# Both S5 layers in finer steps, in a written order for two engines

## The chip, the cores and the metric

The kernel runs on one core of a Trainium2 chip. A core has TensorE (PE, with weight loads listed as PEld), VectorE (DVE), ScalarE (ACT), GpSimd (POOL) and SyncE (SP); each takes its instructions from a queue of its own, in order. SP, ACT and POOL also issue DMAs, and a DMA that waits holds what stands behind it in that queue. The metric is the device time of one execution in microseconds (us).

## The reference

A trunk of four layers over 256 tokens of width 1024 in fp32. Layer i mixes tokens by i mod 3: an S5 state-space layer (layers 0 and 3), forgetting attention (FoX, layer 1), gated linear attention (GLA, layer 2). Each layer is

```python
h += mixer(rmsnorm(h))
h += square(relu(rmsnorm(h) @ w1)) @ w2
h += (p[i] @ W_pp) * sigmoid(rmsnorm(h) @ W_pg)      # PLE
```

and the S5 mixer is

```python
u = xn @ w_in                               # 64 groups of 16 channels
dt = exp(log_dt); ab = exp((lr + 1j * li) * dt)
bbar = (ab - 1) / (lr + 1j * li) * b
s[t] = ab * s[t - 1] + bbar @ u[t]          # 64 complex states a group
y = real(c @ s) + d * u
z1, z2 = split(gelu(y) @ w_glu, 2)
out = (z1 * sigmoid(z2)) @ w_out
```

## The kernel before

Activations lie transposed, features on partitions and the 256 tokens on the free axis. `self.HH` holds h in four tiles of two feature blocks each. A dense product multiplies weights and activations that are split into a high and a low part: `unit` loads 512 KB of weights over SP, ACT makes the high part (L157), VectorE the low part (L159), and `col` issues three matmuls (L173 to L175). A unit is 24 such matmuls. `dense` walks the units of a block of 512 outputs and hands the sums to `evac`. `lo_after` lets a low part wait for an instruction.

**The S5 layer** (`s5`) works in four blocks b of 256 channels (8 pairs of groups). A block's work is:

- w: its part of w_in (`block`, or in layer 0 `plain_block` with plain fp32 weights, L261); then u (L1068), scaled by the row's inverse root mean square `r`; `s5_inputs` spreads u with eight small DMAs, four on SP and four on ACT (L963).
- i: the weights that lead into the states. Layer 0 makes them from `bT` and a table of powers `coef` (L867 to L869), after a rotation `rot` (`s5_rot`, L889 to L892) and the decay `d0` (L1081, L1082).
- o: the weights that lead out (`s5_way_out`, L907 to L911), and `s5_inside`: a small product on TensorE (k, L927 to L932), copied by ACT and spread to `tm`, the lags inside four tokens, by four DMAs on ACT (L942).
- s: `s5_states`: matmuls into the states (L977), rotation (L984 to L986), scan (L989), rotation back (L991 to L1003).
- y: `s5_outputs`: matmuls out (L1015), GELU on ACT, four transposes (L1027) and the split of the result into `g` (L267 on ACT, L268 on VectorE).

In layer 3 the weights of i and o come from DRAM, where `s5_ahead` has put them piece by piece during the MLPs of layers 0 to 2. `s5_scalars` computes the small quantities, as a generator in steps; `s5_table` sends the table to DRAM on POOL's queue and `s5_fetch` brings coef, bT and `bc` back. Step p is `plain_ple_proj` (layer 0) or `ple_proj` (layer 3): the PLE projection of p[i].

The order in which these are traced is the string `FIRST` (layer 0) or `LATER` (layer 3). The last two y are traced inside the first part of the gate. That order isn't the order of execution: the tile framework's planner, which has modelled costs, places each engine's instructions by what it expects to be ready, so steps of several blocks interleave. After the states comes the gate: `dense` for the third block of 512 outputs (`right`: sigmoid on ACT), then the first (`left`: product and split into `m`), then the fourth and the second; then `out_proj`.

PSUM has eight banks, as `acc` (3), `wk` (3), `po` (1) and `mk` (1). Other buffers are counted in `BUFS`.

## Time and profile before

| | us |
|---|---|
| median of 3 runs | 1458.47 |
| lowest, highest | 1456.15, 1462.42 |
| the profiled execution | 1462.34 |
| its span, first to last instruction | 1460.6 |
| S5, layer 0: until the last w_out matmul | 187.4 |
| S5, layer 3: from its first w_in matmul | 1092 to 1239.6 |
| mean granted TensorE clock | 0.982 |

In the profile's tables a group of instructions is named by engine, line, what it writes and reads, and its count. "Idle before" is the time that the engine stood still just ahead of it, with what released it. The ends of matmuls are modelled, since they are pipelined, so TensorE's busy time overstates its work where they are few and small; the start of one step and the start of the next are the better measure.

### The profile page before, as it was taken

How to read it: one execution, taken by the hardware profiler on the slowest of the kernel's cores; microseconds unless marked ns; L12 is line 12 of the kernel's file. 1: busy time of each engine (PE TensorE's matmuls, PEld its weight loads, DVE VectorE, ACT ScalarE, POOL GpSimd, SP SyncE). 2: the span in 40 equal slices, each digit the busy share in tenths (PEclk: the TensorE clock that was granted, in tenths of full speed). 3: DMA queues.
4: the chain of work that ended last, by engine and by line, in shares of the span. 5: the costliest groups of instructions: out<-in, count | busy, mean ns of one | idle time of the engine just before them, and what ended most of it. 6: DMA issues, size and time to landing. Idle time of an engine off the chain costs nothing.

```text
span 1460.6 us, 26531 instructions
## 1 busy us (share of the span) xinstructions
PE 1402.0 (96%) x10734; PEld 1265.4 (87%) x10734; DVE 1050.7 (72%) x1657; ACT 717.5 (49%) x1110; POOL 89.3 (6%) x146
## 2 busy tenths in 40 slices
PE   7799999999999999999999999999997899999998
PEld 6689988889999888888989588888997899888898
DVE  8795578766876678776676468877677856766665
ACT  3133565445655655445566455444463335545453
POOL 4100000001000000010004000100000000000020
PEclk9889999999999999999999999999999899999999
DMA  6634656656654356775655445766665446566561
GB/s 208 191 89 132 181 175 192 189 167 207 191 155 140 122 154 197 242 229 175 186 170 156 134 130 187 229 211 207 204 233 152 145 130 185 181 188 187 173 195 66
DMA packets 146347, 255.06 MB, mean 175 GB/s; under 512 B 24768, under 2 KB 35296, under 8 KB 146224
## 3 DMA queue, kind: packets, MB, share of 16 engines
q1 hardware_dynamic: 132912, 234.35, 52.4%
q0 software_dynamic: 5248, 17.31, 3.7%
q10 hardware_dynamic: 8064, 1.71, 0.6%
q8 instruction: 84, 1.38, 0.4%
q14 instruction: 39, 0.32, 0.1%
HBM read 242.68 MB, written 7.86 MB: 172 GB/s over the span
## 4 chain that ended last, share of the span: by engine, by line
PE 61%; DVE 4%; DMA 2%; ACT 1%; issue 1%; DVEq 0%; POOLq 0%; SPq 0%; ACTq 0%
PE wk L209 8%; PE acc L209 7%; PE acc L173 4%; PE acc L174 4%; PE acc L175 4%; PE wk L211 4%; PE wk L173 4%; PE wk L175 4%; PE wk L174 4%; PE acc L211 3%; PE mk L209 3%; PE po L209 2%; DMA raw<-mlp_w 2%; DVE wlo L159 1%; PE acc L234 1%; PE acc L233 1%
## 5 line engine op out<-in xcount | busy, mean ns | idle before, releaser
L159 DVE TENSOR_TENSOR wlo<-raw,whi 128x1024 fp32r<-128x1024 f32 x406 | 493.6, 1226 | 293.1 <-ACT whi L157 287.5
L157 ACT CAST whi<-raw 128x1024 fp32r<-128x1024 f32 x406 | 421.6, 1049 | 466.1 <-DMA raw<-mlp_w 84.7
L209 PE MATMUL wk<-x,whi 128*128 128x512 f32 x576 | 181.5, 400 | 8.3 <-DVE relu L220 8.3
L211 PEld LDWEIGHTS wk<-x,wlo 128*128 128x128 f32 x576 | 106.4, 190 | 22.8
L209 PE MATMUL acc<-s,whi 128*128 128x512 f32 x384 | 117.7, 395 | 0.0
L211 PE MATMUL wk<-x,wlo 128*128 128x256 f32 x576 | 113.2, 280 | 0.0
L209 PEld LDWEIGHTS wk<-x,whi 128*128 128x128 f32 x576 | 91.8, 191 | 12.3 <-DVE relu L220 9.2
L173 PE MATMUL acc<-x,whi 128*128 128x256 f32 x352 | 99.8, 287 | 1.8 <-DVE u L1068 1.0
L175 PE MATMUL acc<-x,wlo 128*128 128x256 f32 x352 | 100.1, 286 | 0.7 <-DVE wlo L159 0.7
L174 PE MATMUL acc<-x,whi 128*128 128x256 f32 x352 | 99.4, 285 | 0.0
L211 PEld LDWEIGHTS acc<-s,wlo 128*128 128x128 f32 x384 | 69.7, 188 | 15.8 <-DVE wlo L159 0.5
L209 PE MATMUL mk<-x,whi 128*128 128x512 f32 x256 | 81.6, 395 | 0.0
L211 PE MATMUL acc<-s,wlo 128*128 128x256 f32 x384 | 74.3, 281 | 0.1
L175 PE MATMUL wk<-s,wlo 128*128 128x256 f32 x256 | 72.4, 283 | 0.0
L174 PE MATMUL wk<-s,whi 128*128 128x256 f32 x256 | 72.4, 283 | 0.0
L173 PE MATMUL wk<-s,whi 128*128 128x256 f32 x256 | 72.4, 283 | 0.0
L173 PEld LDWEIGHTS acc<-x,whi 128*128 128x128 f32 x352 | 66.9, 191 | 3.3 <-ACT pp L436 1.3
L175 PEld LDWEIGHTS acc<-x,wlo 128*128 128x128 f32 x352 | 67.2, 191 | 1.5 <-DVE wlo L159 1.2
L174 PEld LDWEIGHTS acc<-x,whi 128*128 128x128 f32 x352 | 67.2, 192 | 0.3
L209 PEld LDWEIGHTS acc<-s,whi 128*128 128x128 f32 x384 | 59.7, 189 | 1.6
L209 PE MATMUL po<-s,whi 128*128 128x512 f32 x192 | 60.5, 395 | 0.6 <-DVE y L220 0.6
L209 PE MATMUL wk<-s,whi 128*128 128x512 f32 x192 | 59.6, 395 | 0.0
(398 smaller groups left out, 3368.5 us busy)
## 6 DMA issues: line engine op xcount, KB each, us to landing
raw<-mlp_w SPq DMA_DIRECT2D x256, 512.0 KB, 4.1
raw<-s_w_glu SPq DMA_DIRECT2D x32, 512.0 KB, 3.9
raw<-ple_gate SPq DMA_DIRECT2D x32, 512.0 KB, 3.9
raw<-fox_w_in SPq DMA_DIRECT2D x24, 512.0 KB, 3.8
raw<-gla_w_in SPq DMA_DIRECT2D x24, 512.0 KB, 3.6
raw<-s_w_out SPq DMA_DIRECT2D x16, 512.0 KB, 3.7
kept<-kept SPq DMA_DIRECT2D x12, 512.0 KB, 4.0
raw<-s_w_in SPq DMA_DIRECT2D x11, 512.0 KB, 3.5
```

What stands on the lines that cost most here:

```text
L157: nc.scalar.copy(hi, raw)
L159: self.last_lo = nc.vector.tensor_tensor(lo, raw, hi.bitcast(F32), ALU.subtract)
L173: mm(ps, hi, x[:, 0], start=first, stop=False, skip_group_check=True)
L174: mm(ps, hi, x[:, 1], start=False, stop=False, skip_group_check=True)
L175: self.last_mm = mm(ps, lo, x[:, 0], start=False, stop=last, skip_group_check=True)
L209: mm(ps[n], hi[:, i, s], v[i], start=first and i == 0, stop=False, skip_group_check=True)
L211: self.last_mm = mm(ps[n][:, 0], lo[:, i, s], v[i][:, 0], start=False, stop=last and i == UK - 1, skip_group_check=True)
L233: mm(ps[half], a[:, 0, t], hi[:, k], start=k0 + k == 0, stop=False)
L234: mm(ps[half], a[:, 0, t], lo[:, k], start=False, stop=False)
```

## The change

- `in_order`, a context, links all instructions that are traced inside it on the named engines, each to the one before on the same engine, so that the planner keeps the traced order. `s5` wraps the steps of both layers in it for PE and DVE. ACT, POOL and SP are placed by the planner as before. A few ACT instructions at layer 0's start (the scaled x, the squares and the first steps of the scalars) stand in an order of their own.
- The steps are cut finer: w in halves of a block (w0 to w7), with the weight split of layer 3 as a step (h); u; c (x and squares), n (mean squares), z (inverse root and the rest of the scalars); f and q (fetches), r (rot and decay), i, o, k; x (matmuls into the states), s (rotation and scan), e (rotation back); y, t (transposes, high part), g (low part).
- The gate's right half is no longer done by `dense` after the states. Its eight weight units are steps (l), and a and b are the share of one block of 256 channels in the third and in the fourth 512 outputs: a_b can run once g_b is there. The sigmoids follow the last block, into `self.sg`. The left half follows, both blocks of outputs in a row, its low parts held by `lo_after` until the last g.
- p is `plain_ple_proj` in both layers now, in four parts, with its sums in `po`. The transposes go to `po` as well, y's sums to `mk`, and x's sums always to `wk`.
- Buffers: qo 3 to 2, wt 3 to 4, g2 3 to 2, bx with one of its own.
- `masks` is called in FoX. The zeroing of `tm` and the product `dd` go from POOL to VectorE, `nblk` from POOL to ACT. A Sin of one column is issued early.

```diff
-FIRST = "f0 w0 o0 w1 i0 w2 w3 f1 s0 i1 o1 s1 p0 f2 i2 y0 o2 s2 y1 f3 i3 o3 s3"
-LATER = "w0 i0 o0 w1 i1 o1 w2 s0 i2 w3 s1 p3 y0 o2 s2 i3 y1 o3 s3"
+FIRST = """w0 z0 w1 z1 w2 w3 f1 u0 w4 w5 r0 i0 x0 o0 f2 u1 w6 k0 s0 w7 e0 r1 i1 f3 y0 t0 p0 x1 o1 g0 u2 p1 k1 l0 s1 a0 p2 e1 r2 i2 y1 t1 p3 x2 o2 g1 u3
+k2 l1 l2 s2 b0 a1 e2 y2 l3 r3 i3 t2 b1 x3 o3 g2 k3 l4 l5 s3 a2 b2 e3 l6 y3 t3 g3 a3 l7 b3"""
+LATER = """h0 h1 c0 w0 h2 n0 w1 h3 z0 f0 q0 w2 h4 z1 w3 h5 u0 w4 h6 w5 u1 h7 l0 x0 w6 s0 f1 q1 w7 u2 e0 l1 x1 p0 y0 u3 s1 t0 p1 g0 a0 e1 f2 q2 l2 x2 b0 y1 s2 t1 p2 g1 a1 l3
+e2 f3 q3 x3 p3 y2 b1 s3 t2 g2 l4 a2 l5 e3 b2 l6 y3 t3 g3 a3 l7 b3"""
...
+    @contextmanager
+    def in_order(self, *engines):
+
+        traced = self.nc.cur_bb.bb.instructions
+        before = traced[-1]
+        yield
+        start = next(k for k in reversed(range(len(traced))) if traced[k] is before) + 1
+        for e in engines:
+            last = None
+            for i in [i for i in traced[start:] if i.engine == e]:
+                if last is not None:
+                    self.tc.add_manual_dep(i, last.name, mybir.DependencyInfo(mybir.DependencyClass.NoSync, mybir.DependencyReason.DATA), reason="in_order")
+                last = i
...
     def s5(self, l):
+        nc, A = self.nc, self.A
+        with self.in_order(mybir.EngineType.PE, mybir.EngineType.DVE):
+            gT, last = self.s5_steps(l)
+        m = self.ktiles("glu", tag="m4")
+        self.lo_after = [last]
+        for b, sg in enumerate(self.sg):
...
+            self.dense(gT, A["s5_w_glu"][l // 3], left, (b,), tags=("acc", "wk"))
+        self.lo_after = []
+        self.out_proj(m, A["s5_w_out"][l // 3])
...
+        def z(i):
+            if i == 0:
+                if first:
+
+                    next(v["scalars"])
+                    f(0)
+                    next(v["scalars"])
+                v["rows"] = self.inverse_root(v["ms"])
+                if first:
+                    next(v["scalars"])
+                return
+            v["r"] = self.rstd(v["rows"])
             if first:
-                return self.s5_inside(b, *drain(self.s5_way_out(q, b, parts[b][2])))
...
+                q.update(drain(v["scalars"]))
...
+        def t(b):
+            gT.extend([] if gT else self.ktiles("g"))
+            Gs[b] = self.s5_turn_over(Gs[b], gT[b][:, :, 0])
+
+        def g(b):
+            hi, lo = gT[b][:, :, 0], gT[b][:, :, 1]
+            v["last"] = nc.vector.tensor_tensor(lo, Gs[b], hi.bitcast(F32), ALU.subtract)
...
+        def ahead(i):
+            units[i % 2, i // 2] = self.unit(w_glu[i // 2 * 256:(i // 2 + 1) * 256, (2 + i % 2) * 512:(3 + i % 2) * 512], UK, 512)
+
+        def gate(cb, b):
+            if b == 0:
+                v[cb] = self.banks(("acc", "wk") if cb else ("acc", "acc"))
+            self.pairs(v[cb], gT, *units.pop((cb, b)), 2 * b, b == 0, b == 3)
+            if b == 3:
+                sg = [self.f2("sg") for _ in range(2)]
+                for d, ps in zip(sg, v[cb]):
+                    nc.scalar.activation(d, ps, AF.Sigmoid)
+                self.sg.append(sg)
...
+            with self.in_order(mybir.EngineType.Activation):
+                next(v["scalars"])
+                for kk in range(8):
+                    self.last_x = nc.scalar.activation(x[kk], self.H[kk], AF.Identity, scale=self.gains[:, l, kk:kk + 1])
...
+        steps = dict(h=h, w=w, u=u, c=c, n=n, z=z, f=f, q=q_, r=r, i=i, o=o, k=k, x=x_, s=s, e=e, y=y, t=t, g=g, p=p, l=ahead, a=lambda b: gate(0, b),
+                     b=lambda b: gate(1, b))
+        for step in (FIRST if first else LATER).split():
+            steps[step[0]](int(step[1]))
```

More of the change, by code (lines that the diff above doesn't have):

```diff
@@ L505, in fox @@
         rows = self.rstd_rows(sq)
+        self.masks()
         r = self.rstd(rows)
@@ L1093, in make_out, with h, w @@
[L1093 to L1097 removed]
+        def h(i):
+            units["h", i] = self.unit(w_in[i % 2 * 512:(i % 2 + 1) * 512, i // 2 * 256:(i // 2 + 1) * 256], 4, 256)
+        def w(i):
+            b, i = i // 2, i % 2
+            if i == 0:
+                us[b] = self.psum((128, 2, T), "acc")
+            ps = us[b]
+            if first:
+                raw = self.half(x, w_in, 2 * b + i)
+            else:
+                hi, lo = units.pop(("h", 2 * b + i))
+            for n in range(2):
+                c = slice(n * 128, (n + 1) * 128)
+                for k in range(4):
+                    if first:
+                        nc.tensor.matmul(ps[:, n], raw[:, k, c], x[4 * i + k], start=i == k == n == 0, stop=i == 1 and k == 3, skip_group_check=True)
+                    else:
+                        self.col(ps[:, n], v["x"][2 * i + k // 2][:, k % 2], hi[:, k, c], lo[:, k, c], i == k == n == 0, i == 1 and k == 3)
```

279 lines of the change are left out of this document (131 added, 148 removed).

## The prediction

> **What bounds the kernel now.** I read the page's busy shares first, then busy time by stretches of the span, then who waited for whom, and last the timeline of single steps.
>
> ```profile
> PE 1402.0 (96%) x10734; PEld 1265.4 (87%) x10734; DVE 1050.7 (72%) x1657; ACT 717.5 (49%) x1110; POOL 89.3 (6%) x146
> ```
>
> TensorE is the bound over the span. The change touches two places, so the share has to be read there. In the rows below, which cut the span into stretches, the columns are start:end, length, busy time (instructions) of PE, weight loads, DVE, ACT, POOL, then granted clock, DMA share, GB/s.
>
> ```profile
> 0.00:62.00 62.00, 53.65 (x499) 45.46 (x499) 48.57 (x148) 17.08 (x38) 19.75 (x51) 1.00 0.74 225
> 62.00:92.00 30.00, 19.16 (x235) 15.56 (x237) 29.39 (x38) 7.26 (x13) 0.22 (x2) 0.72 0.20 57
> 92.00:128.00 36.00, 36.00 (x859) 34.69 (x855) 27.43 (x36) 10.89 (x18) 1.10 (x2) 1.00 0.40 114
> 128.00:187.40 59.40, 59.40 (x497) 59.40 (x496) 34.72 (x38) 29.35 (x36) 0.00 (x0) 1.00 0.60 177
> ...
> 1117.00:1179.00 62.00, 47.43 (x789) 44.88 (x788) 48.80 (x60) 16.52 (x24) 0.00 (x0) 0.83 0.43 127
> 1179.00:1239.60 60.60, 60.60 (x508) 60.60 (x506) 35.19 (x38) 30.29 (x37) 0.00 (x0) 1.00 0.59 174
> 187.40:1092.00 904.60, 889.45 (x5810) 789.58 (x5809) 662.83 (x1071) 484.11 (x763) 56.55 (x79) 0.99 0.59 183
> ```
>
> The first S5 layer is 0 to 187.4, the second 1092 to 1239.6. Each falls in two. The state part (to 128, and to 1179) is a chain over four blocks, VectorE to TensorE and back. There TensorE has gaps and a low clock (0.72, 0.83), and VectorE in layer 0 is busy 48.57 + 29.39 + 27.43 = 105.4 of 128 us. The dense part behind it (most of the gate, then w_out) is TensorE without a gap: 497 matmuls in 59.40, 0.12 each. So a gain can come only from work of the dense part that is drawn into the gaps of the state part, and the state part must not get longer for it. In the 904.6 us between, TensorE is 98% busy and the change alters no loop.
>
> The gaps, from the list of waits of TensorE (total, times, longest), and of VectorE and ScalarE up to 130 us:
>
> ```profile
> PE po L1015 <- DVE P L1002: 9.6, 2, 5.4
> ...
> PE acc L454 <- DVE decay L1082: 7.9, 1, 7.9
> ...
> PE acc L977 <- DMA tm<-kept: 3.1, 1, 3.1
> ```
> ```profile
> DVE g L268 <- ACT g L267: 8.0, 2, 6.1
> DVE wh L867 <- DMA U<-u: 5.4, 1, 5.4
> ```
> ```profile
> ACT decay L1081 <- DMA U<-u: 14.1, 1, 14.1
> ```
>
> TensorE's long waits are few, and a slow clock follows them: 0.72 is the mean of the 30 us that hold the 7.9.
>
> **The change part by part.** *Steps in a written order.* No instruction of the four-block chain goes away; its order on PE and DVE is now fixed. I price a step by where it starts and where the next one starts. First VectorE (columns: start, length, engine, line, what it does):
>
> ```profile
> 29.87 1.20 DVE L889 TENSOR_TENSOR rot<-F,F 128x1024 f32<-128x1024 f32 x1
> ...
> 54.90 1.04 DVE L1068 TENSOR_TENSOR u<-acc,rstd 128x512 f32<-128x512 f32 x1
> ...
> 62.40 1.23 DVE L867 TENSOR_TENSOR wh<-bT,coef 128x1024 f32<-128x1024 f32 x1 [5.42 <-DMA U<-u]
> ...
> 64.75 1.22 DVE L984 TENSOR_TENSOR W<-wk,rot 128x1024 f32<-128x1024 f32 x1
> ...
> 77.72 0.66 DVE L997 SCALAR_TENSOR_TENSOR W<-R,rot 128x504 f32<-128x504 f32 x1
> ...
> 80.01 2.35 DVE L889 TENSOR_TENSOR rot<-F,F 128x1024 f32<-128x1024 f32 x2
> ...
> 83.60 1.49 DVE L907 TENSOR_TENSOR scratch<-bc,cpow 128x1280 f32<-128x1280 f32 x1
> ...
> 89.19 1.48 DVE L907 TENSOR_TENSOR qo<-bc,cpow 128x1280 f32<-128x1280 f32 x1
> ...
> 93.59 0.68 DVE L268 TENSOR_TENSOR g<-acc,g 128x512 fp32r<-128x512 f32 x1
> 94.19 1.21 DVE L984 TENSOR_TENSOR P<-wk,rot 128x1024 f32<-128x1024 f32 x1
> ...
> 100.42 0.67 DVE L997 SCALAR_TENSOR_TENSOR W<-R,rot 128x504 f32<-128x504 f32 x1
> ...
> 101.00 3.49 DVE L159 TENSOR_TENSOR wlo<-raw,whi 128x1024 fp32r<-128x1024 f32 x3
> ```
>
> So u is 1.0, i 64.75 - 62.40 = 2.35, e 80.01 - 77.72 = 2.3, r 3.6, o 93.59 - 89.19 = 4.4, g 0.6, s 100.42 - 94.19 less 0.25 idle = 5.9, and a weight's low half (l) 1.16. Then TensorE:
>
> ```profile
> 37.83 3.72 PE L261 MATMUL acc<-x,wh 128*128 128x256 f32 x16
> ...
> 53.26 0.39 PE L927 MATMUL mk<-zero 1*32 1x512 bf16 x1
> ...
> 55.48 0.40 PE L932 MATMUL mk<-dd,ident 32*32 32x128 f32 x2
> ...
> 59.69 1.99 PE L454 MATMUL acc<-praw,raw 128*128 128x256 f32 x8
> 69.60 3.78 PE L454 MATMUL acc<-praw,raw 128*128 128x256 f32 x8 [7.91 <-DVE decay L1082]
> ...
> 110.41 1.15 PE L1015 MATMUL po<-tm,U 64*64 64x64 f32 x32
> ...
> 115.22 0.38 PE L173 MATMUL wk<-g,whi 128*128 128x256 f32 x1
> ...
> 117.83 0.60 PE L1027 MATMUL acc<-ident,G 128*128 128x128 f32 x4
> ...
> 1156.92 2.08 PE L977 MATMUL acc<-U,kept 64*64 64x64 f32 x64
> ```
>
> In layer 0 half a block of w_in (w) is 3.6, k 55.48 + 0.4 - 53.26 = 2.6, p 1.9, y 115.22 - 110.41 = 4.8, t 0.4, and x twice the last row (two terms per part), 3.7. A gate unit (a, b) is 24 matmuls by 0.12 = 2.9. In layer 3, x is 2.0, y 2.9, w 2.9 and e 3.5 (four operations, of 1.13, 1.13, 0.6 and 0.6 as their like above).
>
> *Layer 0, walked through.* What the walk needs beside the rows: the scalars end near 24 us, since the first rot, which needs all of them, began at 29.87 with o0 (4.4) and u0 (1.0) already done ahead of it; both now come later. Then u0, r0, i0, o0, u1 (12.4) end at 36. TensorE does w0 to w5 meanwhile and x0 at 36 to 39.7, so s0 is done at 44.4 and e0 at 46.7. The next wait is new: y0 needs k0's lags, which go out by DMA, and ACT issues them.
>
> ```profile
> 63.63 2.52 ACTq L942 DMA_DIRECT2D tm<-kk  x4
> ```
> ```profile
> tm<-kk ACTq DMA_DIRECT2D x2, 48.0 KB, 5.7
> ...
> tm<-kk ACTq DMA_DIRECT2D x2, 32.0 KB, 2.0
> ```
>
> k0 ends at 45.9; copy 0.6, four issues 2.5, landing 5.7 (I take the long one while the DMA share is 0.74, and 2.0 for later blocks): y0 at 54.7 to 59.5. Behind y0 in TensorE's queue stand t0, p0, x1. p0 shares one buffer ("po") with t0, so it waits until VectorE has read that in g0 (63.0); x1 ends at 68.5, s1 at 73.2, y1 at 82.8, x2 at 92.0, s2 at 96.7, y2 at 105.2, x3 at 112.8, s3 at 119.3, e3 at 121.6, y3 at 126.4, g3 at 128.6. That is no earlier than the 128.1 (127.4 + 0.7) of before. But all of the gate's right half except a3 and b3 (two units, 5.8) is then done, and what is left behind g3 is 5.8 + 384 matmuls by 0.12 = 46.0, so 51.8 in place of 187.4 - 128.1 = 59.3. Layer 0 ends at 180.4: **7.0 less.** Nothing is faster in the state part; the dense part has lost 7.5.
>
> *Layer 3.* TensorE's queue is w0, then n0 (mean squares), then w1, so w1 can no longer run ahead of n0. These rows of VectorE end what n0 needs:
>
> ```profile
> 1096.49 1.29 DVE L479 TENSOR_TENSOR h<-h,z 128x512 f32<-128x512 f32 x2
> ...
> 1102.15 0.68 DVE L310 TENSOR_TENSOR sq<-sq 128x512 f32<-128x512 f32 x1
> ```
>
> Of two L159 operations that lie between them one can move behind, so n0 starts at 1101.5, and TensorE, done with w0 at 1095, idles 6.5 us where before it ran w_in. That is a wait the change adds, and behind it stands every later matmul. w1 then runs at half clock for some 3.4 us (as L454 x8, 3.78 behind the wait of 7.9 and 1.99 before it) and ends at 1106.7; x0 ends at 1120.4, s0 at 1125.2, y0 at 1132.9, g0 at 1138.1 (p1 waits for it), s2 at 1149.4, y2 at 1164.0, e3 at 1174.4, g3 at 1180.6, b3 at 1186.4. With 46.0 behind it the layer ends at 1232.5 to 1233: **6.6 less** than 1239.6. The plain projection is in this: 32 passes by 0.23 = 7.4 on TensorE for 48 by 0.12 = 5.8, +1.6, and 3 us of VectorE less.
>
> *Edits with the answer "nothing".* masks goes from layer 0 to FoX, into time of POOL, which is 6% busy; nblk to ACT; the Sin table is loaded while ACT waits for h. If that cover fails it is about 1.3 us once. dd and the three memsets move from POOL to VectorE; the trace has no such row on VectorE. Bounds: 0 (they fit before 2.5 us or into waits) and 2.6 (POOL's times); I take 1. Fewer buffers (qo, g2, one bx): in the walk no step asks for one before its reader is done, so 0; the upper end is one wait of a buffer for a block, 5 us, as in the U wait above.
>
> **Sum.** 1462.3 (the profiled execution, span 1460.6) - 7.0 - 6.6 = 1448.7. The median shown, 1458.5, is 3.9 lower, so the forecast is **1445**.
>
> **The rivals.** *Packed (1424).* tm lands early, and the scheduler finds room for w0 inside the PLE gate. Layer 0's floor is VectorE: 105.4 + 1.2 (a seventh l before g3) + 1 + 2.5 until the first input + 6 for y3, t3 after e3 = 116, and 51.8 behind it: 168, 19 less. Layer 3's floor is TensorE, about 122 us of matmuls from 1092 plus some 9 for n0: 1223, 16 less. For: VectorE's work fits. Against: each block ends in a round trip.
>
> *Waits only move (1458).* The order holds, but the gate units wait for g of their block while the block behind waits for them; the 13.6 us goes in four to six new waits of 2 to 3 us. This is also where "it does not do what it says" ends: ACT, SP and POOL are still ordered by the planner, so the two fixed queues can stand before an unfixed one. For: ACT sat 14.1 us behind U transfers. Against: x(b) comes 10 us or more after u(b) in the walk.
>
> *Slower: late lags (1473).* Place: y(b) in layer 0, at the head of TensorE's queue, t, p and x of the next block behind it. The issues wait in ACT's queue, which the wait of 14.1 shows held up once. If k(b) to y(b) costs 5.3 more in each of four blocks, that is 21, plus 1.8 for each slow clock afterwards (3.78 less 1.99), 28 in all: 1445 + 28 = 1473. It decides from about 3 us per block on, where the 13.6 is eaten.
>
> *Slower: the clock sinks (1483).* The rows show it falling after waits of 3 us and more and staying at 1.00 in 92 to 128, where waits are short. If short waits cost clock as well, at 0.74 the matmuls of the state parts (about 64 in layer 0 from y0 on, 76 in layer 3) would take 49 us more, of which gaps hide 11: 1445 + 38 = 1483. The Trainium skill, "TensorE: Matmul & The Clock Gate", section "A second HAM failure mode: psum-queue depth-cycling", says that frequent micro-idles between matmul groups make the clock swing. By that page this rival is the outcome, by the 1.00 of 92 to 128 it is not.
>
> **How the numbers follow.** Forecast (1436 to 1452) 0.50; packed 0.18; waits only move 0.18; late lags 0.10; clock 0.04. A measurement of this kernel can tell about 0.5% (7.3 us) from no change. Faster by more, under 1451.2: 0.18, and nearly all of the forecast case, 0.50 + 0.18 + a little = 0.70. Within: 0.16. Slower, over 1465.8: 0.14. The range takes in the packed case at its centre and the moved waits with a buffer wait on top, 1424 to 1464; outside are the two slower cases and the lower half of packed.
>
> **What would show it.** Right: PE's sum of matmul time unchanged but for 1.6 us; in 128 to 187 some 8 us less of dense work behind the last g; "acc L454 <- decay" gone; a new wait of wk L321 on DVE sq near 1100; y waits for tm. Wrong: DVE waiting over 15 us in 25 to 128 for anything but x and y; granted clock under 0.9 in the state parts; g3 later than 135; or a change in the 904.6 us between the layers.

## The result, and the profile after

| | before | after |
|---|---|---|
| median (us), four runs each, side by side | 1457.88 | 1479.18 |
| lowest, highest | 1456.15, 1462.42 | 1477.72, 1483.93 |
| ratio of the times, 95% interval | | 1.0147 (1.0113 to 1.0181) |
| the profiled execution; its span | 1462.34; 1460.6 | 1480.56; 1478.9 |

The changed kernel is slower by 1.5%, 21 us. Forecast were 1445 us and a gain. The busy shares of the page barely move, so they can't tell why:

```profile
PE 1407.8 (95%) x10718; PEld 1268.7 (86%) x10718; DVE 1051.8 (71%) x1659; ACT 715.7 (48%) x1109; POOL 85.1 (6%) x140
```

To find the place, cut both executions where the last addition to h of each stage ends. These two rows of VectorE in the changed kernel close the two S5 layers (start, length, engine, line, operation):

```profile
190.67 1.42 DVE L287 TENSOR_TENSOR h<-h,wk 128x512 f32<-128x512 f32 x2
...
1257.39 1.42 DVE L287 TENSOR_TENSOR h<-h,wk 128x512 f32<-128x512 f32 x2
```

| stage | ends, before | ends, after | the stage itself |
|---|---|---|---|
| S5, layer 0 | 188.3 | 192.1 | +3.8 |
| MLP 0 | 374.6 | 383.0 | +4.6 |
| PLE 0 to PLE 2 | 1097.8 | 1106.0 | -0.2 |
| S5, layer 3 | 1240.5 | 1258.8 | +10.1 |
| MLP 3, PLE 3 | 1449.9 | 1468.2 | 0.0 |

So three stages lose, 18.5 us together. By medians the loss is 21.3, between the two profiled executions 18.2: that of before was itself 4.5 above its median, that of after 1.4. A stage that no edit touches differs between executions, too. The -0.2 holds +3.1 in GLA and -2.1 in MLP 1, and over all the versions below MLP 1 takes 189.0 to 193.1. Three of them run layer 3 with every engine's instructions and transfers in the same order, and it takes 136.2, 139.2 and 140.2. Each version has one profiled execution, so a difference of a single stage under 4 us is not read as an effect, unless a wait in the rows or several versions together show it. For the two S5 layers, the busy time by stretches (columns as in the prediction), before and then after:

```profile
8.00:188.30 180.30, 165.79 (x2072) 152.87 (x2073) 136.81 (x243) 60.06 (x95) 15.75 (x30) 0.95 0.54 160
1097.80:1240.50 142.70, 126.47 (x1440) 123.40 (x1439) 97.38 (x116) 55.27 (x72) 0.72 (x1) 0.93 0.51 152
```
```profile
8.00:192.10 184.10, 168.61 (x2080) 155.90 (x2081) 139.80 (x247) 58.51 (x92) 11.74 (x25) 0.96 0.51 154
1106.00:1258.80 152.80, 131.10 (x1447) 125.80 (x1448) 96.77 (x115) 52.41 (x68) 1.63 (x1) 0.91 0.49 152
```

Length less TensorE's busy time is its idle time. In layer 3 it rises from 16.2 to 21.7, and the matmuls themselves take 4.6 more at a lower granted clock (0.91 for 0.93). In layer 0 it is 14.5 before and 15.5 after: the change was to fill those gaps, and they are as large as they were. The waits of TensorE over the whole span of the changed kernel (total, times, longest) show what they consist of now:

```profile
PE po L441 <- DVE g L1192: 13.6, 4, 8.4
...
PE po L1029 <- ACT G L1022: 7.7, 7, 2.5
...
PE mk L1013 <- DMA tm<-kk: 6.7, 3, 4.3
PE wk L321 <- DVE sq L308: 5.9, 1, 5.9
PE acc L225 <- ACT whi L173: 3.5, 1, 3.5
```

The 7.9 us behind VectorE's decay, the 9.6 behind its P and the 3.1 for tm<-kept of before are gone; these stand in their place. Three chains in the timeline show how they come about.

*Layer 0, the last block.* ScalarE's queue, and then TensorE's and VectorE's:

```profile
123.48 1.05 ACT L173 CAST whi<-raw 128x1024 fp32r<-128x1024 f32 x1 [9.01 <-DMA raw<-s_w_glu]
...
125.62 0.56 ACT L926 COPY kk<-mk 32x512 f32<-32x512 f32 x1
126.20 2.49 ACTq L934 DMA_DIRECT2D tm<-kk  x4
```
```profile
130.22 1.58 PE L1013 MATMUL mk<-tm,U 64*64 64x64 f32 x32 [4.34 <-DMA tm<-kk]
```
```profile
138.64 0.69 DVE L1192 TENSOR_TENSOR g<-po,g 128x512 fp32r<-128x512 f32 x1 [8.95 <-ACT g L1030]
```

ScalarE stood 9 us at the cast of a gate weight that was still loading; the copy of kk3 came behind it, then the lags by DMA, and y3, next in TensorE's fixed queue, waited 4.3 us. g3 ends at 139.3, the walk had it at 128.6.

*Layer 0, the clock behind the waits.* Three parts of the projection, of eight like matmuls each: p0 behind the two waits around t0, the next without a wait, and p3 behind a wait. Then three stretches that follow waits of TensorE (p0 and x1 behind g0, p3 and x2 behind g1, y3 behind its lags):

```profile
59.44 0.66 PE L1029 MATMUL po<-ident,G 128*128 128x128 f32 x4 [0.69 <-ACT G L1022]
...
61.63 3.02 PE L441 MATMUL po<-praw,raw 128*128 128x256 f32 x8 [1.54 <-DVE g L1192]
...
69.03 1.99 PE L441 MATMUL po<-praw,raw 128*128 128x256 f32 x8
...
87.40 3.78 PE L441 MATMUL po<-praw,raw 128*128 128x256 f32 x8 [2.20 <-DVE g L1192]
```
```profile
61.60:69.10 7.50, 7.47 (x137) 6.41 (x137) 3.21 (x3) 0.58 (x1) 0.00 (x0) 0.77 0.54 147
87.40:96.00 8.60, 8.60 (x137) 7.34 (x137) 4.31 (x4) 1.18 (x2) 0.00 (x0) 0.66 0.59 162
130.20:136.70 6.50, 6.43 (x160) 6.31 (x160) 0.00 (x0) 1.07 (x2) 0.00 (x0) 0.74 0.27 86
```

The granted clock is 0.77, 0.66 and 0.74 there. The walk priced p and x together at 1.9 + 3.7 and y at 4.8, so the three stretches hold 6.5 of the 10.7 us by which g3 is late.

*Layer 3, block 0.* ScalarE's transposed copy of g0 stands behind four U issues that took 7.0 us; TensorE's next instruction, p1, shares the bank "po" with it and waits for VectorE's g0 behind that copy:

```profile
1146.69 7.02 ACTq L955 DMA_DIRECT2D U<-u  x4
1153.76 0.58 ACT L1030 CAST g<-po 128x512 fp32r<-128x512 f32 x1 [7.79 <-DMA U<-u]
```
```profile
1155.12 2.50 PE L441 MATMUL po<-praw,raw 128*128 128x256 f32 x5 [8.44 <-DVE g L1192]
```

*MLP 0*, which the change does not touch in code. The buffers `wt` hold bT and coef, the S5 parameters of a block of 256 channels. Between 320 and 352 us of the changed kernel, and 316 and 350 of the one before, the DMA issues of POOL that bring S5 parameters for layer 3 (count, KB each, median us to landing) are

```profile
bT<-s_bT POOLq DMA_DIRECT2D x2, 512.0 KB, 5.9
coef<-tab POOLq DMA_DIRECT2D x4, 256.0 KB, 9.5
```
```profile
coef<-tab POOLq DMA_DIRECT2D x2, 256.0 KB, 5.4
bT<-s_bT POOLq DMA_DIRECT2D x1, 512.0 KB, 5.6
```

Two blocks go out in one piece instead of one, and in the changed kernel a weight block of the MLP comes late under them:

```profile
345.64 1.04 ACT L173 CAST whi<-raw 128x1024 fp32r<-128x1024 f32 x1 [9.24 <-DMA raw<-mlp_w]
```
```profile
346.74 1.65 PE L225 MATMUL acc<-s,whi 128*128 128x512 f32 x3 [3.46 <-ACT whi L173]
```

### The profile page after: what moved, and what is told of

It reads as the page before. It is cut to its first block, busy times and chain, and to the rows that moved or that the text cites. A ratio compares the mean times of both kernels' runs of the same rounds, so it can differ in the third digit from the quotient of the medians.

```text
span 1478.9 us, 26478 instructions
## 1 busy us (share of the span) xinstructions
PE 1407.8 (95%) x10718; PEld 1268.7 (86%) x10718; DVE 1051.8 (71%) x1659; ACT 715.7 (48%) x1109; POOL 85.1 (6%) x140
## 4 chain that ended last, share of the span: by engine, by line
PE 59%; DVE 3%; DMA 3%; ACT 2%; issue 1%; POOL 1%; ACTq 0%; DVEq 0%; POOLq 0%; SPq 0%
PE wk L225 8%; PE acc L225 7%; PE wk L227 4%; PE wk L189 4%; PE wk L190 4%; PE wk L191 4%; PE acc L189 3%; PE acc L227 3%; PE acc L190 3%; PE acc L191 3%; PE mk L225 3%; PE po L225 2%; DVE wlo L175 2%; DMA raw<-mlp_w 1%; PE mk L227 1%; PE acc L250 1%
## 5 line engine op out<-in xcount | busy, mean ns | idle before, releaser
L189 PE MATMUL acc<-x,whi 128*128 128x256 f32 x352 | 101.4, 291 | 0.8 <-ACT pp L423 0.8
L225 PEld LDWEIGHTS wk<-x,whi 128*128 128x128 f32 x576 | 91.7, 190 | 11.2 <-DVE relu L236 8.1
L190 PE MATMUL acc<-x,whi 128*128 128x256 f32 x352 | 100.8, 287 | 0.0
L227 PEld LDWEIGHTS acc<-s,wlo 128*128 128x128 f32 x384 | 70.5, 190 | 15.5
```

Of the source, the lines that this page charges most:

```text
L189: mm(ps, hi, x[:, 0], start=first, stop=False, skip_group_check=True)
L190: mm(ps, hi, x[:, 1], start=False, stop=False, skip_group_check=True)
L225: mm(ps[n], hi[:, i, s], v[i], start=first and i == 0, stop=False, skip_group_check=True)
L227: self.last_mm = mm(ps[n][:, 0], lo[:, i, s], v[i][:, 0], start=False, stop=last and i == UK - 1, skip_group_check=True)
```

## The experiments

Theory A came first: TensorE and VectorE are fixed, ScalarE is still ordered by the planner, and its waits for transfers stand ahead of the short copies that the fixed queues need next. Others followed. All runs start from the changed kernel unless it is said otherwise. "Layer 3" below is the time from the last addition of PLE 2 to the last of layer 3; g3 is the start of VectorE's last low part of layer 0. The stages are those of the one profiled execution of each version. For pe_only that was the slowest of its four, 9.9 us above their median.

| run | median us | ratio to before (95%) | layer 0 ends | g3 | MLP 0 | layer 3 |
|---|---|---|---|---|---|---|
| before | 1457.88 to 1460.34 | 1 | 188.3 | 127.4 | 186.3 | 142.7 |
| after | 1479.18 | 1.0147 (1.0113 to 1.0181) | 192.1 | 138.6 | 190.9 | 152.8 |
| act_order | 1512.00 | 1.0352 (1.0319 to 1.0384) | 221.2 | 163.7 | 189.7 | 159.7 |
| planner_order | 1463.54 | 1.0026 (1.0010 to 1.0042) | 189.6 | 136.5 | 189.1 | 142.3 |
| wt3 | 1476.76 | 1.0100 (1.0061 to 1.0139) | 188.3 | 134.9 | 187.9 | 155.4 |
| u_by_sp | 1477.43 | 1.0106 (1.0065 to 1.0148) | 195.8 | 142.2 | 191.7 | 150.0 |
| pe_only | 1488.60 | 1.0207 (1.0166 to 1.0249) | 200.1 | 145.1 | 191.5 | 156.6 |
| dve_only | 1467.61 | 1.0053 (1.0030 to 1.0075) | 193.1 | 140.0 | 191.9 | 139.2 |
| casts_n0 | 1475.99 | 1.0110 (1.0081 to 1.0139) | 194.8 | 139.9 | 188.4 | 149.3 |
| planner_wt3 | 1464.64 | 1.0030 (1.0009 to 1.0051) | 191.0 | 137.9 | 186.8 | 141.4 |
| p_bx | 1470.21 | 1.0070 (1.0046 to 1.0095) | 190.6 | 137.1 | 188.6 | 149.6 |
| mended | 1468.58 | 1.0062 (1.0041 to 1.0084) | 189.6 | 134.7 | 189.0 | 147.8 |
| l3_dve_only | 1459.45 | 1.0007 (0.9992 to 1.0021) | 189.4 | 135.9 | 187.2 | 136.2 |
| fill_free | 1461.49 | 1.0014 (1.0005 to 1.0024) | 188.4 | 135.3 | 185.1 | 142.6 |
| l6_usp | 1462.72 | 1.0020 (1.0006 to 1.0034) | 189.8 | 134.9 | 187.0 | 139.3 |
| new_l3_alone | 1455.45 | 0.9975 (0.9958 to 0.9993) | 189.0 | 128.1 | 185.8 | 140.2 |
| casts_behind_g3 | 1459.07 | 0.9998 (0.9986 to 1.0009) | 187.8 | 130.6 | 186.9 | 139.1 |

### Which queue is fixed

**act_order**: ScalarE follows the written order too.

```diff
-        with self.in_order(mybir.EngineType.PE, mybir.EngineType.DVE):
+        with self.in_order(mybir.EngineType.PE, mybir.EngineType.DVE, mybir.EngineType.Activation):
```

> The changed kernel with ScalarE's queue, too, held to the written order inside both S5 layers. Theory A (ScalarE's queue, which the planner still orders, holds instructions that wait for a transfer or a buffer ahead of the short copies that the fixed TensorE and VectorE queues need next): the last block's VectorE piece g3 of layer 0 comes at 129 to 133 instead of 138.6, that of layer 3 about 5 us earlier than the 93 us after the layer's first sum that the changed kernel took, and the whole kernel takes 1463 to 1472 us. Theory B (the written order of TensorE and VectorE is itself poor, whatever ScalarE does): g3 stays at 137 or later and the whole stays at 1476 or more.

1512 us: 33 slower than the changed kernel. Theory A's remedy makes it worse, in layer 0 above all (+29). Who waited there, between 20 and 222 us, TensorE and then VectorE:

```profile
PE acc L189 <- ACT whi L173: 16.1, 6, 5.2
```
```profile
DVE wlo L175 <- ACT whi L173: 64.5, 20, 15.3
```

Both wait for casts of gate weights, 16.1 and 64.5 us. The written order puts these casts behind the copies and the lag transfers of the block, so ScalarE makes them only when the gate is next, where the planner had put them into its waits (18.5 us for VectorE in the changed kernel). An order that suits TensorE and VectorE is no order for a queue that also casts and issues transfers. That the three disagree is therefore not the whole cause.

**planner_order**: nothing is fixed; all other edits stay.

```diff
-        with self.in_order(mybir.EngineType.PE, mybir.EngineType.DVE):
+        with nullcontext():
```

> The changed kernel without any written order: the fine steps stay, but the planner orders TensorE and VectorE as well as ScalarE. Theory A (three queues out of step): the queues agree again, TensorE's waits for ScalarE and for the lag transfers fall below 2 us each in the state parts, g3 of layer 0 near 130, the whole 1460 to 1470 us. Theory B (the fine steps and the buffers cost the time, not the fixing of two queues): the whole stays at 1474 to 1485 us. In both, MLP 0 keeps its 5.3 us of loss.

1463.5 us, 0.26% above before: layer 3 gives back all of its 10.1, layer 0 2.5 of its 3.8. MLP 0 keeps 2.8 of 4.6. In layer 3 fixing costs the time, not the finer steps; but these alone bring nothing either. For layer 0 it is not shown: with three wt buffers (below) the fixed order takes 188.3 and the planned one 191.0. In layer 0 TensorE still waits once 4.1 us for tm and once 6.7 for g, so the expected fall of single waits under 2 us did not come.

**pe_only** and **dve_only**: one engine is fixed, the other planned.

```diff
-        with self.in_order(mybir.EngineType.PE, mybir.EngineType.DVE):
+        with self.in_order(mybir.EngineType.PE):
```
```diff
-        with self.in_order(mybir.EngineType.PE, mybir.EngineType.DVE):
+        with self.in_order(mybir.EngineType.DVE):
```

> The changed kernel with the written order kept for TensorE alone, VectorE planned. Theory P (TensorE's fixed queue costs the time: it stands at a matmul whose operand is late while others are ready): the S5 layers stay as long as in the changed kernel (layer 0 about 192 us at its last sum, layer 3 about 153 us from sum to sum), the whole 1474 to 1482. Theory D (VectorE's fixed queue costs it: pieces of state work stand behind pieces that wait for ScalarE): layer 0 falls to 189 to 190 and layer 3 to 142 to 144 us, the whole 1461 to 1468. If only both together cost, it lies with this as well as with its counterpart near 1464.

> The changed kernel with the written order kept for VectorE alone, TensorE planned. Theory D: layers 0 and 3 stay at about 192 and 153 us, the whole 1474 to 1482. Theory P: 189 to 190 and 142 to 144 us, the whole 1461 to 1468.

Theory P holds in layer 3, and more sharply than put: with TensorE alone fixed it takes 156.6, with VectorE alone 139.2, less than the 142.7 of before. The slow execution of pe_only can be a part of its 156.6; with both fixed, the layer takes 152.8 and 155.4 in executions near their medians. In layer 0 the two differ by 7 (200.1 and 193.1), but neither beats both fixed (192.1). Layer 3 of the two runs, in stretches, pe_only and then dve_only:

```profile
1119.70:1276.30 156.60, 133.92 (x1447) 128.19 (x1448) 94.14 (x113) 52.99 (x69) 0.72 (x1) 0.89 0.45 142
```
```profile
1105.40:1244.60 139.20, 127.97 (x1442) 121.86 (x1442) 96.63 (x115) 52.66 (x68) 1.64 (x1) 0.98 0.54 167
```

TensorE's idle time is 22.7 against 11.2, its clock 0.89 against 0.98, and the same matmuls take 133.9 against 128.0 us. So in these two executions 11.5 us of idle time cost 17.4.

### What in TensorE's order costs layer 3

**casts_n0** (with three wt buffers, see below): n0 goes behind w1. Its layer 0 part is read further below.

```diff
-h0 h1 c0 w0 h2 n0 w1 h3 z0
+h0 h1 c0 w0 h2 w1 h3 n0 z0
```

> Three wt buffers, and two edits that are read apart because they lie in different layers. In layer 0 the casts of the last four gate units stand behind the copy of the last block's lag matrices in ScalarE's queue: theory A (a cast that waits for its weights holds up that copy) expects TensorE's wait of 3.8 us for tm ahead of y3 gone and g3 at 131 to 133 instead of 134.9, the layer's end 2 to 4 us earlier; the rival (VectorE is busy without a break from 98 to 125 us and sets e3, so that y3 ends where it did) expects g3 within 1 us of 134.9. In layer 3 step n0 stands two weight steps later: theory N (the wait of 5.9 us for the sum of squares is a pure loss) expects 4 to 6 us off the layer; the rival (the weight steps then wait for their casts, or the state work that follows waits longer) 0 to 2. The whole 1467 to 1471 us if both theories hold, 1474 to 1477 if neither.

Layer 3 falls from 155.4 (wt3) to 149.3, and the wait of 5.9 at L321 is gone: theory N. The fall is 6.1 against wt3 and 3.5 against the changed kernel, which runs layer 3 in the same order as wt3. The forecast had this wait (6.5 us, measured 5.9) as part of a gain; a planned queue never has it.

**p_bx**: n0 as in casts_n0, without the edit of the casts; besides, p1 and p2 stand ahead of y0 and y1.

```diff
-x1 p0 y0 u3 s1 t0 p1 g0 a0 e1
+x1 p0 p1 y0 u3 s1 t0 g0 a0 e1
...
-b0 y1 s2 t1 p2 g1 a1 l3
+b0 p2 y1 s2 t1 g1 a1 l3
...
-"bx": 1,
+"bx": 2,
```

> Three wt buffers, both queues in the written order, n0 two weight steps later, and two more edits read apart by layer. Layer 3: the pieces p1 and p2 of the projection go ahead of y0 and y1 instead of behind t0 and t1. Theory P (TensorE stands at p because its bank is still read by VectorE's g): the 8.3 us of TensorE's waits for g at the projection go, and the layer falls from 149.3 to 142 to 146 us. Rival (the gate step behind p waits for the same g): the wait moves to the gate, the layer stays at 148 to 150. Layer 0: two bx buffers instead of one; the 16.3 us in which ScalarE waits for the first bx go, the copy kk0 comes as soon as TensorE's k0 is done. Theory A: y0 1 to 2 us earlier and g0 at 58 to 60 instead of 60.4, the layer 1 to 3 us shorter; rival: no change over 1 us, since ScalarE waited for the same TensorE step either way.

149.6 for 149.3: the 8.3 us wait for g at the projection goes and comes back one step earlier, at the transposes:

```profile
1146.06 1.11 PE L1029 MATMUL po<-ident,G 128*128 128x128 f32 x4 [6.72 <-ACT G L1022]
```

The rival named the wrong place (the gate), but its size was right: nothing is gained. Two bx buffers in layer 0 bring g0 from 60.4 to 59.5, and the layer nothing (190.6, where wt3 took 188.3).

**u_by_sp** and **mended**: all U by SP, so that ScalarE's copies stand behind none.

```diff
-            queue = self.nc.scalar if p % 2 else self.nc.sync
-            queue.dma_start(U[:, p], u[p % 4 * 32:p % 4 * 32 + 32, p // 4].rearrange("x (s j) -> x s j", s=4))
+            self.nc.sync.dma_start(U[:, p], u[p % 4 * 32:p % 4 * 32 + 32, p // 4].rearrange("x (s j) -> x s j", s=4))
```

mended does so in layer 3 alone, on top of p_bx, and in layer 0 lets VectorE copy the decay:

```diff
-            nc.scalar.copy(d0, (q["r4"] if first else self.kept[1])[:, b * 8:(b + 1) * 8].unsqueeze(2).broadcast_to([128, 8, 64]))
+            (nc.vector.tensor_copy if first else nc.scalar.copy)(d0, (q["r4"] if first else self.kept[1])[:, b * 8:(b + 1) * 8].unsqueeze(2).broadcast_to([128, 8, 64]))
```

> The changed kernel with all eight U transfers of a block issued by SP, none by ScalarE. Theory A: ScalarE no longer stands behind U issues that wait; in layer 3 the copy of g0 comes 7 us earlier (45 us after the layer's first sum where it took 52), the layer is 4 to 7 us shorter, layer 0 by 0 to 3; the whole 1470 to 1476 us. Rival (SP's queue has weight blocks that wait for their buffers ahead of U, so that U itself comes late): x of a block waits for U by 2 to 8 us longer, the whole 1480 to 1495 us.

> As the run with p and bx, and with two more edits. Layer 3: all U transfers issued by SP, so that ScalarE's copy of g0 stands behind none of them; theory A 3 to 5 us off the layer beside that run (139 to 143 us in all, below the 142.7 of the kernel before), rival 0 to 1. Layer 0: the decay tile is copied by VectorE instead of ScalarE: VectorE's waits of 2.5 us for it go for 0.6 us of work per block; theory 1 to 3 us off the layer beside that run, rival (VectorE is busy without a break where the state is made) 0 to 2 us longer.

g0 of layer 3 comes 43.3 us after PLE 2 instead of 48.4, which is theory A's direction with 5.1 for its 7. The layer itself falls by 2.8 (152.8 to 150.0), and by 1.8 in mended (149.6 to 147.8), less than theory A had and no more than executions differ. Layer 0 is 3.7 longer with U on SP alone, where 0 to 3 less was expected. The decay on VectorE brings g3 of layer 0 2.4 earlier (137.1 to 134.7), the 2.5 that VectorE waited for it, and the layer's end 1.0.

With n0, p and U mended, layer 3 is still at 147.8 against 136.2 to 140.2 with TensorE planned, and so these three places together do not explain the loss. The timelines show what the rest is. TensorE around t0 (transposes, L1029) with its queue planned (**l3_dve_only**, below), and in the changed kernel:

```profile
1138.02 0.63 PE L967 MATMUL wk<-U,kept 64*64 64x64 f32 x16
1138.89 0.66 PE L1029 MATMUL po<-ident,G 128*128 128x128 f32 x4 [0.23 <-ACT G L1022]
1139.47 0.92 PE L1013 MATMUL mk<-tm,U 64*64 64x64 f32 x24
1140.22 1.10 PE L967 MATMUL wk<-U,kept 64*64 64x64 f32 x32
1141.15 0.40 PE L1013 MATMUL mk<-tm,U 64*64 64x64 f32 x8
1142.46 0.62 PE L189 MATMUL acc<-g,whi 128*128 128x256 f32 x3 [0.91 <-ACT g L1030]
```
```profile
1142.79 1.51 PE L1013 MATMUL mk<-kept,P 64*64 64x64 f32 x46
1146.02 0.66 PE L1029 MATMUL po<-ident,G 128*128 128x128 f32 x4 [1.73 <-ACT G L1022]
```

Behind the last row the fixed queue has p1 at 1155.12, shown above, after 8.4 us of nothing.

The planner cuts the steps: pieces of the next block's x, of its lags' y and of the gate lie between y0, t0 and a0, so a hand-over to ScalarE costs 0.2 to 0.9 us. In the fixed queue each step is one block, and nothing fills its hand-overs.

**fill_free** tests this. VectorE is fixed; on TensorE only the chain (lags, x, y, t) is, while w, n, p, a and b are the planner's.

```diff
-            for i in [i for i in traced[start:] if i.engine == e]:
+            for i in [i for i in traced[start:] if i.engine == e and not (e == mybir.EngineType.PE and i.name in self.fill)]:
...
+            n0 = len(nc.cur_bb.bb.instructions)
             steps[step[0]](int(step[1]))
+            if step[0] in "wnabp":
+                self.fill |= {ins.name for ins in nc.cur_bb.bb.instructions[n0:]}
```

> Three wt buffers, VectorE in the written order in both layers, and TensorE's written order kept for the chain of the states alone (lags, way in, outputs, transposes), while the dense fill (input products, mean squares, gate, projection) is left to the planner. Theory F (the fixed order costs because the fill can no longer be slid into the gaps between pieces of the chain): layer 3 comes to 136 to 142 us, as with TensorE planned, where both queues fixed took 155.4; layer 0 to 178 to 184 us from its eighth microsecond, where both fixed took 180.3. Rival G (the chain's own pieces, each issued as one block, cost the time): layer 3 stays at 147 us or more.

142.6, just above theory F's 142 and far under rival G's 147: freeing the fill gives back 12.8 of the 155.4. Freeing the chain as well gives another 2.4 to 6.4 (140.2, 139.2, 136.2), which is hardly more than executions differ. So the fill is the larger part, and rival G's part stays open. In layer 0 freeing the fill brings nothing: 188.4, or 180.4 from its eighth microsecond, where both fixed took 180.3. The whole is at 1461.5, from 1476.8.

**l3_dve_only**: three wt buffers, both queues fixed in layer 0, VectorE's alone in layer 3.

```diff
+        with self.in_order(*([mybir.EngineType.PE] * (l == 0)), mybir.EngineType.DVE):
```

> Three wt buffers; layer 0 with both queues in the written order, layer 3 with VectorE's alone. Theory P (in layer 3 it is TensorE's fixed queue that costs): layer 3 takes 139 to 142 us as with VectorE's order alone everywhere, layer 0 stays at 188 to 192, the whole 1454 to 1461 us, within 0.4% of the kernel before. Rival (layer 3's gain there came of what preceded it): layer 3 at 143 or more, the whole 1462 to 1470.

Layer 3 takes 136.2, the forecast's -6.6 (142.7 to 136.2 is -6.5) from a kernel that isn't the one of the forecast. That it is the same size is luck: the same order took 139.2 in dve_only and 140.2 in new_l3_alone. The whole is where before is. TensorE's idle time in the layer is 8.6:

```profile
1100.20:1236.40 136.20, 127.63 (x1443) 122.00 (x1443) 96.71 (x116) 52.55 (x68) 1.63 (x1) 0.97 0.54 171
```

**l6_usp** adds U by SP in layer 3 to this: 139.3 for 136.2. That is no gain, and no loss can be read from it either: casts_behind_g3 has the layer 3 of l3_dve_only in its code and takes 139.1. With TensorE planned, little waits for that copy. Its expectation and its part in layer 0 follow.

### Layer 0 and the last block

casts_n0 also put the casts of the last four gate units behind the copy kk3 (with i >= 4), l6_usp only those of the last two (i >= 6):

```diff
+            with self.tc.issue_after(self.cast_after.ins) if self.cast_after else nullcontext():
+                nc.scalar.copy(hi, raw)
...
+            self.cast_after = self.last_kk if first and i >= 6 else None
```

> Three wt buffers, both queues fixed in layer 0, VectorE's alone in layer 3. Layer 0: only the casts of the last two gate units stand behind the copy kk3 in ScalarE's queue (four did in an earlier run, and the layer grew by 6.5 us). Theory A: TensorE's 3.8 to 4.2 us wait for tm ahead of y3 falls under 2 us, g3 1 to 3 us earlier than 134.9, the layer's end at 186 to 188; rival (VectorE's queue, and not the copy, sets y3): 188 to 191. Layer 3: U issued by SP alone. Theory A: 1 to 3 us less than the 136.2 us that this layer took without it; rival (with TensorE planned, nothing waits for that copy): within 1 us of 136.2.

With four casts held the layer grew by 6.5. With two, TensorE's wait for tm fell to 1.8, and g3 is at 134.9 all the same. ScalarE's queue in l6_usp:

```profile
118.84 0.56 ACT L929 COPY kk<-mk 32x512 f32<-32x512 f32 x1
...
131.54 1.04 ACT L176 CAST whi<-raw 128x1024 fp32r<-128x1024 f32 x1 [6.80 <-DMA raw<-s_w_glu]
132.50 0.59 ACT L1025 ACTIVATE G<-mk 128x512 f32<-128x512 f32 x1
```

kk3 comes 3 us earlier than in wt3 (121.87), but the cast that waits for its weights now stands ahead of G3. So **casts_behind_g3** put both casts behind ScalarE's last copy of g, and step l6 behind g3:

```diff
-e3 l6 y3 t3 g3 a3 l7 b3
+e3 y3 t3 g3 l6 a3 l7 b3
...
+            self.cast_after = self.last_hi if first and i >= 6 else None
```

> Three wt buffers, both queues fixed in layer 0, VectorE's alone in layer 3. In layer 0 the casts of the last two gate units stand behind ScalarE's copy of the last block's high part, and their step l6 behind g3 in the written order, so that nothing that waits for weights stands ahead of kk3, G3 or that copy. Theory A (in layer 0 a cast that waits for its weights always stands ahead of one of ScalarE's short copies; with the casts behind kk3 it was G3): g3 at 130 to 132.5 instead of 134.9 to 135.9, ScalarE's wait for weights no longer ahead of G3; the layer ends at 185 to 188 if the dense rest behind g3 stays near 53 us. Rival (VectorE's chain sets e3 and y3, or the rest behind g3 grows by what g3 wins, since the weight units come later): g3 under 132.5 but the end at 188 to 191, or g3 at 134 or later.

```profile
128.67 0.60 ACT L1024 ACTIVATE G<-mk 128x512 f32<-128x512 f32 x1 [10.02 <-PE mk L1015]
130.01 0.59 ACT L1032 CAST g<-po 128x512 fp32r<-128x512 f32 x1 [0.75 <-PE po L1031]
```

g3 at 130.6, as theory A had it: the queue did hold it. But the layer ends at 187.8, only 1.6 before l3_dve_only, since 57.2 us stand behind g3 now instead of 53.5. From g3 to the layer's end, l3_dve_only and then casts_behind_g3:

```profile
135.90:189.40 53.50, 53.12 (x437) 52.81 (x438) 34.66 (x38) 26.53 (x33) 0.00 (x0) 1.00 0.60 188
```
```profile
130.60:187.80 57.20, 55.74 (x437) 55.34 (x438) 35.80 (x39) 30.40 (x37) 0.00 (x0) 0.94 0.59 185
```

TensorE does the same 437 matmuls in both. Of the 3.7 us more, 2.6 are the clock (0.94 for 1.00) and 1.1 is idle time, most of it a wait of 1.6 for the casts that were held back. So ScalarE's queue sets g3, and 3.7 of the 5.3 us won there are lost again behind it. TensorE's idle time in layer 0 is 12.4 us here, 14.5 before, and 13 to 20 in all other versions but act_order (34.6).

### The losses outside the two layers

**wt3**: three wt buffers, as before.

```diff
-"wt": 4,
+"wt": 3,
```

> The changed kernel with three wt buffers in place of four. Theory C (the fourth buffer lets two blocks of S5 parameters, 2.2 MB instead of 1.2, go out in one piece during MLP 0, so that a weight block of the MLP comes late): the 9.2 us wait of ScalarE for raw and the 3.46 us of TensorE after it are gone, MLP 0 takes about 5 us less, the S5 layers change by under 2 us each, the whole 1473 to 1476 us. Rival (the MLP's loss comes of the shifted phase of its weight stream, not of the buffer): the wait stays, the whole 1477 to 1482 us; and if block 1's coefficients come late for lack of the buffer, layer 0 is up to 4 us longer.

MLP 0 falls by 3.0 (190.9 to 187.9); TensorE's wait there is 1.5 instead of 3.5, and POOL sends in the same stretch

```profile
coef<-tab POOLq DMA_DIRECT2D x2, 256.0 KB, 6.7
```

in place of four (bT stays at two). One pair of executions would not show 3.0 us, but the versions together do: MLP 0 takes 189.1 to 191.9 in the six with four wt buffers, 185.1 to 189.0 in the nine with three, 185.8 and 186.3 in the two with the layer 0 of before. ScalarE's long wait for raw did not go, as expected, but shrank from 9.2 to 7.3. Layer 0 is 3.8 shorter, which was not expected. TensorE, VectorE, ScalarE and SP have the same order there in both kernels. POOL sends coef of two blocks at once with four buffers, and VectorE's wait for the first coef is 2.5 us with four and 0.6 with three. The rest of the 3.8 is not traced. Layer 3 took 2.6 more in the same order, which is no effect of the buffer.

**planner_wt3**: three buffers and no order.

> Three wt buffers and no written order: both suspected costs out, the fine steps, the block-by-block gate, the narrow buffers and the plain projection in layer 3 stay. Theory: the losses add, so the loss of 2.8 us in MLP 0 of the planned version goes too: the whole 1456 to 1461 us, within 0.3% of the kernel before, that is, the new steps themselves bring nothing that can be measured. Rival: the new steps are worth the 7 us per layer forecast once nothing holds them: 1445 to 1452.

1464.6, no better than planner_order (1463.5), although MLP 0 is back at 186.8 (before 186.3): layer 0 (+1.4), MLP 1 (+2.8) and MLP 2 (+2.0) took what it won, none of them by more than executions differ. The finer steps by themselves bring nothing.

**new_l3_alone**: the kernel before, with its own layer 0 and buffers, and the changed layer 3 (`s5_new` is the changed `s5`) with VectorE's order alone.

```diff
     def s5(self, l):
+        if self.kept is not None:
+            return self.s5_new(l)
```

> The kernel before, with its own buffers and its own layer 0, and the changed layer 3 with VectorE's order alone. If layer 3's gain stands by itself and the losses of MLP 0 hang on the changed layer 0 and its buffers: layer 3 takes 136 to 139 us where the kernel before took 142.7, nothing else moves by over 1 us, the whole 1453 to 1456 us, 0.3 to 0.5% faster than before. Rival (the finer layer 3 needs the narrower buffers, or its gain is lost to what it changes in MLP 2): 1458 to 1464.

1455.45 us, ratio 0.9975 (0.9958 to 0.9993): the one version that is faster than both kernels, by a quarter of a per cent. It is one of sixteen versions and its interval ends close to 1, so the gain is weakly shown. MLP 0 is as before (185.8), so its loss hangs on the changed layer 0 and its buffers. Layer 3 takes 140.2, less than before, and 4.0 more than in l3_dve_only with the same order.

## Why the prediction was wrong

- **The share that bounds, and where to look: right.** TensorE's gaps in the state parts were the only thing to win. The waits of before went as said, and the dense rest behind g3 shrank as worked out: 51.8 forecast, 190.7 - 139.3 = 51.4 measured.
- **The walk through layer 0: this step failed.** It let the state part hold three more units and end where it ended before (g3 at 128.6); g3 ended at 139.3. Two terms were left out. First the clock: the walk has TensorE wait for g0 and g1 and then prices p, x and y at full clock, though its own rows show the same eight matmuls at 3.78 us behind a wait and 1.99 without. Three stretches at a granted clock of 0.66 to 0.77 took 6.5 us more than priced. Second ScalarE's queue: it had "copy 0.6, four issues 2.5, landing 5.7", a ScalarE that starts a copy when its input is there. VectorE waited 2.5 for a decay that stood behind the GELU of y2, and y3 began 1.7 after e3 because kk3 stood behind a cast. By steps, y2 ends 4.1 later than walked, s3 6.8, y3 10.2, g3 10.7. casts_behind_g3 shows the last block's part of the queue (g3 4 to 5 us earlier); the clock's part is read from the rows and no run isolates it. That y0 agrees (53.9 for 54.7) is luck: the scalars ended at 27.3 instead of 24, and the lags landed in 1.9 instead of 5.7.
- **"Nothing is faster in the state part; the dense part has lost 7.5": counted as a gain, it was a move.** The gate units that leave the dense part need TensorE ahead of g3. Only a fall in idle time by as much would have made them free. It went from 14.5 to 15.5, and busy time from 165.8 to 168.6.
- **Layer 3: n0 right, what follows wrong.** Its wait is there (5.9 of 6.5 us). The walk did have a hand-over behind y0, 5.2 us from y0 to g0, but again with a ScalarE that starts at once. Counted from the end of PLE 2, s0 came 4.9 later than walked, g0 8.8 (its copy stood behind U issues of 7.0), s2 10.9 and g3 14.8. Measured, the layer took 10.1 more where 6.6 less was forecast. The walk takes the order as written and has no price for a fill that can't move up when a hand-over is late: with VectorE fixed, a fixed TensorE queue costs 13.6 us (152.8 and 139.2) to 19.2 us (155.4 and 136.2) against a planned one.
- **"Edits with the answer nothing": right but for one.** The finer steps, bx, qo and g2, masks and the plain projection together cost 0.3% (planner_wt3, 1.0030 of the time before). But only *fewer* buffers were weighed. The one that grew (wt) let POOL send 1 MB more in one piece, in a stage that the sum had at zero.
- **The rivals.** "Waits only move" named the mechanism, that "the two fixed queues can stand before an unfixed one", and its end in new waits; its price, nothing gained and nothing lost, had no term for the fill that can't move, for the slow clock or for MLP 0. "Late lags" had its place right for y3, but 4.3 of the 6.7 us were one block, held by a cast of weights and not by U. "The clock sinks" did not come in its size: the mean clock of layer 0 is 0.96 after 0.95 before, and no row has its 0.74 for a whole state part. But its condition came in part, since p0 ran slow (3.02 us) behind waits of 0.7 and 1.5, where the prediction read it as falling after 3 us and more. In layer 3 it is 0.91 after 0.93; its matmuls take 4.6 us more, 1.6 of which were forecast for the projection, so that some 3 of the 10.1 are the clock's. The Trainium skill, "TensorE: Matmul & The Clock Gate", section "A second HAM failure mode: psum-queue depth-cycling", has, for another kernel, the clock swing and throughput fall where TensorE idles briefly but often between groups of matmuls. The trace agrees in layer 3 (0.89 with 22.7 us idle in pe_only, 0.98 with 11.2 in dve_only) and in the three stretches of layer 0.
- **What would show it** was named on both sides. Of the right signs most came: the dense work behind g3 fell, the wait for the decay went, the one for sq came. They speak of the place, not of the time. Of the wrong signs came g3 later than 135 (138.6), a clock under 0.9 in a state part (0.89 in layer 3 up to its g3), and a change between the layers (+4.4 by the stages' ends).

Still open: what wt does to layer 0 beside the wait for coef, how much the slow clock alone costs in layer 0, and how much of that layer's idle time, 12 us at best, any order could fill. No version brought layer 0 under 187.8, where before took 188.3.

## What to carry to other kernels

A fixed queue stands at its next instruction, however late the operand. Before fixing one, walk every queue that its instructions wait for; here fixing ScalarE as well made it worse. In layer 3 a planner that slides dense work into hand-overs matmul by matmul did more than a list of steps, so hold the chain on the engine that makes it and leave the engine that fills to the planner. When work is moved from a stretch that an engine fills into one with gaps, the gain is the fall in that engine's idle time, not what the first stretch loses: work out both, and price matmuls behind a wait at the clock that the rows show there. A ScalarE that casts weights is a queue with transfers in it; walk it like the others, and price a buffer that grows by what it lets go out earlier. Read one stage of one execution against a second execution of the same order first.

## What the runs showed of the hardware

- Four small U transfers took 3.24 us to issue on ScalarE's queue at 1140.2 us, and 7.02 at 1146.7, where transfers of 512 KB had just been issued by SP. ScalarE's next copy stood behind them for 7.8 us. What the issues waited for, the rows don't name. The Trainium skill, "DMA: Bandwidth & Descriptors", section "Issuing engines are not separate DMA queues", has it that issuing on several engines saves only the sequencer's time, usually a small part of the transfer. Here that time counted for ScalarE's own work, since with all U on SP the copy of g0 came 5.1 us earlier. At the layer's end 2.8 were left, no more than executions differ.
- For the same matmuls of layer 3, 11.5 us more idle time came with 5.9 us more busy time and a clock of 0.89 for 0.98 (pe_only, in its slowest execution, and dve_only). Idle time of TensorE was dearer than its length.
- A slow stretch of TensorE can follow waits as short as 0.7 and 1.5 us, within 3 us of each other: the eight matmuls of p0 behind them took 3.02 us, eight like ones 1.99.
